# One DMA ring for the loads and the stores of an RMSNorm-SiLU kernel

## The chip, the cores and the metric

One core of a Trainium2 chip. The metric is the device time of one execution in microseconds (us). The span that a profile shows is 1.7 to 2.1 us shorter than the timed execution of the same run. All runs told here are listed as fast, but for three of the four of lockstep, which are listed as slow for their time alone: the granted clock was 1.0 in every run. Ratios are the mean time of one kernel's fast runs over that of the other kernel's fast runs of the same rounds, so they are not quite the ratios of the medians that I quote.

## The reference

```python
def reference(x, gamma, eps):                 # x: 8 x 1024 x 2048 float32, gamma: 2048
    rms = np.sqrt(np.mean(x ** 2, axis=-1, keepdims=True) + eps)
    out = gamma * x / rms
    return (out * (1 / (1 + np.exp(-out)))).astype(np.float32)
```

64 MiB come in and 64 MiB go out, and each element is touched by a handful of operations.

## The kernel before

The 8192 rows are 16 blocks of 512 rows. A block is a tile of 128 partitions with 4 rows (32 KB) each, 4 MiB in all. Six tiles rotate, so block b+6 uses the memory of block b, and its load has to wait for the store of block b.

```python
    BUFS = 6
    def load(b):
        xt = pool.tile([P, J * d], f32, name="xt")
        nc.scalar.dma_start(out=xt, in_=xb[b])          # ScalarE's queue
        blocks[b] = xt

    def squares_scalar(b, loads=()):
        ...                                              # ScalarE: Square with a row sum
                for s in loads:
                    load(s)                              # b + 3, between two squares

    def store(b):
        nc.sync.dma_start(out=ob[b], in_=blocks[b])      # SyncE's queue
    ...
        for b in range(BUFS):
            load(b)
    ...
        nc.sync.dma_start(out=grow[0:P:P // Q, :], ...)  # gamma's row
        ...                                              # TensorE spreads it, VectorE copies it to g
    ...
        for b in range(last):
            loads = [b + 3] if BUFS <= b + 3 < nblk else []
            ...                                          # squares, root, multiply, Silu, store(b)
```

ScalarE and VectorE share the squares, ScalarE takes the root and the Silu, VectorE the reciprocal and the multiplications. I call a DMA queue of one issuing engine a ring, since its transfers are served in order; load b is L(b), store b is S(b).

Of the kernel before, what the change touches and what calls it, by code (L numbers as in the profile page):

```python
# [1 line left out]

# [4 lines left out]

ACT = mybir.ActivationFunctionType
ALU = mybir.AluOpType


@with_exitstack
def kernel(
    ctx: ExitStack,
    tc: tile.TileContext,
    x: bass.AP,
    gamma: bass.AP,
    eps: bass.AP,
    out: bass.AP,
):  # L20





    nc = tc.nc
    P = nc.NUM_PARTITIONS
    f32 = mybir.dt.float32
    x2 = x.flatten_outer_dims()
    o2 = out.flatten_outer_dims()  # L30
    n, d = x2.shape
    J = 4
    BUFS = 6
    nblk = n // (P * J)
    xb = x2.rearrange("(b p j) d -> b p (j d)", p=P, j=J)
    ob = o2.rearrange("(b p j) d -> b p (j d)", p=P, j=J)

    singles = ctx.enter_context(tc.tile_pool(name="singles", bufs=1))
    pool = ctx.enter_context(tc.tile_pool(name="pool", bufs=BUFS))
    small = ctx.enter_context(tc.tile_pool(name="small", bufs=2))  # L40
    psum = ctx.enter_context(tc.tile_pool(name="psum", bufs=1, space=bass.MemoryType.PSUM))

    Q = 4
    w = d // Q
    grow = singles.tile([P, w], f32)
    g = singles.tile([P, d], f32)
    eps_t = singles.tile([P, 1], f32)
    ones = singles.tile([P, P], f32)
    junk_a = psum.tile([P, d], f32, name="junk_a")
    junk_v = psum.tile([P, d], f32, name="junk_v")  # L50
    blocks, sss, rmss, rstds = {}, {}, {}, {}

    def load(b):
        xt = pool.tile([P, J * d], f32, name="xt")
        nc.scalar.dma_start(out=xt, in_=xb[b])  # L55
        blocks[b] = xt

    def row(b, j):
        return blocks[b][:, j * d:(j + 1) * d]

    def squares_scalar(b, loads=()):


        sss[b] = small.tile([P, J], f32, name="ss")
        for j in range(share(b)):
            nc.scalar.activation(out=junk_a, in_=row(b, j), func=ACT.Square,  # L66
                                 accum_out=sss[b][:, j:j + 1])
            if j == 0:
                for s in loads:
                    load(s)  # L70

    def squares_vector(b):
        for j in range(share(b), J):
            nc.vector.tensor_tensor_reduce(  # L74
                out=junk_v, in0=row(b, j), in1=row(b, j), scale=1.0, scalar=0.0,
                op0=ALU.mult, op1=ALU.add, accum_out=sss[b][:, j:j + 1])

    def share(b):
        return 1 if 4 <= b <= 12 and b % 2 == 0 else 2

    def root(b):
        rms = small.tile([P, J], f32, name="rms")
        nc.scalar.activation(out=rms, in_=sss.pop(b), func=ACT.Sqrt, scale=1.0 / d, bias=eps_t)  # L83
        rmss[b] = rms

    def invert(b):
        rstd = small.tile([P, J], f32, name="rstd")
        nc.vector.reciprocal(out=rstd, in_=rmss.pop(b))  # L88
        rstds[b] = rstd

    def multiply(b):
        for j in range(J):
            nc.vector.scalar_tensor_tensor(out=row(b, j), in0=row(b, j), scalar=rstds[b][:, j:j + 1],  # L93
                                           in1=g, op0=ALU.mult, op1=ALU.mult)

    def silu(b):
        for h in range(0, J, 2):
            cols = slice(h * d, (h + 2) * d)
            nc.scalar.activation(out=blocks[b][:, cols], in_=blocks[b][:, cols], func=ACT.Silu)  # L99
        store(b)  # L100

    def store(b):
        nc.sync.dma_start(out=ob[b], in_=blocks[b])

    with tc.manual_schedule():

        for b in range(BUFS):
            load(b)
        nc.vector.memset(ones, 1.0)  # L109
        nc.vector.memset(eps_t, float(eps))  # L110
        nc.scalar.activation(out=junk_a[:, 0:1], in_=ones[:, 0:1], func=ACT.Square)  # L111
        nc.sync.dma_start(out=grow[0:P:P // Q, :],
                          in_=bass.AP(tensor=gamma.tensor, offset=gamma.offset, ap=[[w, Q], [1, w]]))
        for c in range(Q):
            k = c * (P // Q)
            nc.tensor.matmul(junk_v[:, c * w:(c + 1) * w], ones[k:k + 1, :], grow[k:k + 1, :],  # L116
                             start=True, stop=True)
        nc.vector.tensor_copy(out=g, in_=junk_v)  # L118



        last = nblk - 1
        SOON = 3
        squares_scalar(0)
        squares_vector(0)
        root(0)
        invert(0)
        for b in range(last):
            loads = [b + 3] if BUFS <= b + 3 < nblk else []
            if b < SOON:  # L130
                multiply(b)
                squares_scalar(b + 1, loads)
                silu(b)
                squares_vector(b + 1)
                root(b + 1)
            elif b < last - 1:
                squares_scalar(b + 1, loads)
                squares_vector(b + 1)
                root(b + 1)
                multiply(b)  # L140
                silu(b)
            else:
                multiply(b)
                squares_scalar(b + 1)
                silu(b)
                squares_vector(b + 1)
                root(b + 1)
            if b + 1 < last:
                invert(b + 1)


        for j in range(J):
            if j == J // 2:
                invert(last)
            nc.vector.tensor_mul(out=row(last, j), in0=row(last, j), in1=g)  # L155
        for j in range(J):
            nc.scalar.activation(out=row(last, j), in_=row(last, j), func=ACT.Silu,  # L157
                                 scale=rstds[last][:, j:j + 1])
        store(last)


# [1 line left out]
_INS = ['x', 'gamma', 'eps']  # L163
_OUTS = [((8, 1024, 2048), 'float32')]

_NUMBERS = {'eps': 9.999999747378752e-06}


# [26 lines left out]
```

## Time and profile before

| | before |
|---|---|
| time | 316.92 us (316.83 to 317.22); the profiled run 316.84 us |
| span in the profile | 315.1 us |
| VectorE, ScalarE busy | 75%, 68% |
| DMA engines busy, both rings | 99.0% |
| rate, over the span | 426 GB/s |

The page of the profile cuts the span into 40 slices, with a digit for the busy tenths of each engine and of the sixteen DMA engines, and the GB/s moved. The lines are in the prediction below. One more view of it matters later: the issues by kind, with the median time from issue to landing in the last column.

```profile
xt<-in_x_dram ACTq DMA_DIRECT2D x16, 4096.0 KB, 38.7
out_dram<-xt SPq DMA_DIRECT2D x16, 4096.0 KB, 29.0
```

### The profile page before, as it was taken

Reading aid. Unit: us, or ns where it says so; the run is one execution under the profiler, and the core shown is the slowest. Engines: PE = TensorE matmul, PEld = TensorE weight load, DVE = VectorE, ACT = ScalarE, POOL = GpSimd, SP = SyncE. Lnnn points to the kernel's source line nnn. Section 1 sums busy time; section 2 is a strip of 40 time slices with the busy share of each in tenths; the row PEclk is TensorE's granted clock in tenths of the full one; section 3 lists DMA queues with packets and bytes.
Section 4 is the critical chain, followed back from the end, with each engine's and each line's share of the span. In section 5 each row is a group of like instructions: output and inputs, shape, how many; then the busy total and the mean of one; then the engine's idle time right before and its main releaser. Section 6 shows DMA issues by size and latency. Waiting matters only on the chain.

```text
span 315.1 us, 436 instructions
## 1 busy us (share of the span) xinstructions
PE 2.1 (1%) x8; PEld 0.5 (0%) x8; DVE 235.3 (75%) x157; ACT 213.8 (68%) x136; POOL 0.2 (0%) x4
## 2 busy tenths in 40 slices
PE   0200000000000000000000000000000000000000
PEld 0000000000000000000000000000000000000000
DVE  0679597979995695957969489693995939999600
ACT  1349998972799258682687827877288768779910
POOL 0000000000000000000000000000000000000000
DMA  8999999999999999999999999999999999999996
GB/s 334 403 462 403 395 466 399 466 403 462 403 463 403 459 412 453 412 453 420 445 420 445 424 441 424 441 424 441 428 437 437 428 445 420 445 420 445 420 449 287
DMA packets 4618, 134.24 MB, mean 426 GB/s; under 512 B 516, under 2 KB 516, under 8 KB 520
## 3 DMA queue, kind: packets, MB, share of 16 engines
q10 hardware_dynamic: 2304, 67.11, 49.7%
q1 hardware_dynamic: 2312, 67.12, 49.3%
q14 instruction: 2, 0.02, 0.0%
HBM read 67.12 MB, written 67.11 MB: 426 GB/s over the span
## 4 chain that ended last, share of the span: by engine, by line
DMA 68%; DVE 14%; ACT 11%; issue 2%; ACTq 1%; DVEq 0%
DMA xt<-in_x_dram 68%; DVE xt L93 9%; DVE junk_v L74 5%; ACT xt L99 4%; ACT junk_a L66 3%; ACT xt L157 2%; ACT L83 1%; ACTq L190 1%; ACT L157 0%; ACT L99 0%; ACT rms L83 0%; DVE ss L74 0%; DVE rstd L88 0%; ACTq L55 0%; ACTq L83 0%
## 5 line engine op out<-in xcount | busy, mean ns | idle before, releaser
L93 DVE SCALAR_TENSOR_TENSOR xt<-xt,rstd,g 128x2048 f32<-128x2048 f32 x60 | 137.0, 2347 | 0.1
L99 ACT ACTIVATE xt<-xt 128x4096 f32<-128x4096 f32 x30 | 108.3, 3615 | 27.2 <-DVE xt L93 27.1
L74 DVE CUSTOM_DVE_ANT_0 junk_v<-xt 128x2048 f32<-128x2048 f32 x37 | 85.1, 2299 | 42.5 <-DMA xt<-in_x_dram 41.7
L66 ACT ACTIVATE junk_a<-xt 128x2048 f32<-128x2048 f32 x27 | 50.7, 1877 | 22.6 <-DMA xt<-in_x_dram 22.3
L83 ACT ACT_TABLE_LOAD x15 | 19.2, 1283 | 27.6 <-DVE ss L74 27.5
L99 ACT ACT_TABLE_LOAD x14 | 18.0, 1283 | 0.2
L118 DVE COPY g<-junk_v 128x2048 f32<-128x2048 f32 x1 | 2.3, 2292 | 9.4 <-PE junk_v L116 9.4
L88 DVE RECIPROCAL rstd<-rms 128x4 f32<-128x4 f32 x16 | 2.8, 174 | 8.3 <-ACT rms L83 8.3
L155 DVE TENSOR_TENSOR xt<-xt,g 128x2048 f32<-128x2048 f32 x4 | 8.9, 2279 | 0.0
L83 ACT ACTIVATE rms<-ss,eps_t 128x4 f32<-128x4 f32 x16 | 4.8, 297 | 5.7 <-DVE ss L74 5.5
L157 ACT ACTIVATE xt<-xt,rstd 128x2048 f32<-128x2048 f32 x4 | 7.7, 1990 | 0.0
L74 DVE DVE_READ_ACCUMULATOR2_ANT ss<- 128x1 f32 x37 | 5.2, 141 | 0.0
L66 ACT ACTIVATION_READ_ACCUMULATOR junk_a<-xt 128x1 f32 x27 | 5.0, 186 | 0.0
L111 ACT ACT_TABLE_LOAD x1 | 1.3, 1283 | 3.8 <-issue 3.8
L116 PE MATMUL junk_v<-grow,ones 1*128 1x512 f32 x8 | 2.1, 1130 | 8.2 <-DMA grow<-in_gamma_dram 8.2
L157 ACT ACT_TABLE_LOAD x1 | 1.3, 1283 | 0.0
L109 DVE MEMSET ones<- 128x128 f32 x1 | 0.2, 165 | 0.8 <-PEq L176 0.8
L116 PEld LDWEIGHTS junk_v<-grow,ones 1*128 1x128 f32 x8 | 0.5, 307 | 8.2 <-issue 8.2
L111 ACT ACTIVATE junk_a<-ones 128x1 f32<-128x1 f32 x1 | 0.2, 174 | 0.0
L176 POOL MEMSET const-bfloat16-1.0<- 128x1 bf16 x1 | 0.1, 101 | 0.0
L176 POOL MEMSET const-uint8-127<- 128x1 uint8 x1 | 0.1, 101 | 0.0
L176 POOL MEMSET const-float32-0.0<- 128x1 f32 x1 | 0.1, 98 | 0.2 <-issue 0.2
(2 smaller groups left out, 0.2 us busy)
## 6 DMA issues: line engine op xcount, KB each, us to landing
xt<-in_x_dram ACTq DMA_DIRECT2D x16, 4096.0 KB, 38.7
out_dram<-xt SPq DMA_DIRECT2D x16, 4096.0 KB, 29.0
grow<-in_gamma_dram SPq DMA_DIRECT2D x1, 8.0 KB
```

The source lines that it names most:

```text
L66: nc.scalar.activation(out=junk_a, in_=row(b, j), func=ACT.Square, accum_out=sss[b][:, j:j + 1])
L74: nc.vector.tensor_tensor_reduce(out=junk_v, in0=row(b, j), in1=row(b, j), scale=1.0, scalar=0.0, op0=ALU.mult, op1=ALU.add, accum_out=sss ...
L83: nc.scalar.activation(out=rms, in_=sss.pop(b), func=ACT.Sqrt, scale=1.0 / d, bias=eps_t)
L88: nc.vector.reciprocal(out=rstd, in_=rmss.pop(b))
L93: nc.vector.scalar_tensor_tensor(out=row(b, j), in0=row(b, j), scalar=rstds[b][:, j:j + 1], in1=g, op0=ALU.mult, op1=ALU.mult)
L99: nc.scalar.activation(out=blocks[b][:, cols], in_=blocks[b][:, cols], func=ACT.Silu)
L111: nc.scalar.activation(out=junk_a[:, 0:1], in_=ones[:, 0:1], func=ACT.Square)
L116: nc.tensor.matmul(junk_v[:, c * w:(c + 1) * w], ones[k:k + 1, :], grow[k:k + 1, :], start=True, stop=True)
L118: nc.vector.tensor_copy(out=g, in_=junk_v)
L155: nc.vector.tensor_mul(out=row(last, j), in0=row(last, j), in1=g)
L157: nc.scalar.activation(out=row(last, j), in_=row(last, j), func=ACT.Silu, scale=rstds[last][:, j:j + 1])
L190: with _tile.TileContext(nc) as tc:
```

## The change

Its intent is that ScalarE no longer issues big loads between its squares, and that loads go out as soon as their memory is free. All loads and stores go to SyncE. Behind S(b), from block 1 on, stands L(b+5), which waits for S(b-1) to land. ScalarE issues gamma's row, now straight into g without the tile grow, and nothing else.

```diff
     def load(b):
         xt = pool.tile([P, J * d], f32, name="xt")
-        nc.scalar.dma_start(out=xt, in_=xb[b])
+        nc.sync.dma_start(out=xt, in_=xb[b])
 ...
-    def squares_scalar(b, loads=()):
+    def squares_scalar(b):
 ...
-            if j == 0:
-                for s in loads:
-                    load(s)
 ...
     def store(b):
         nc.sync.dma_start(out=ob[b], in_=blocks[b])
+        if b >= 1 and b + BUFS - 1 < nblk:
+            load(b + BUFS - 1)
 ...
+        nc.scalar.dma_start(out=g[0:P:P // Q, 0:w], ...)      # gamma's row
-        nc.sync.dma_start(out=grow[0:P:P // Q, :], ...)
```

The squares, roots, multiplications and Silus keep their order.

More of the change, by code (lines that the diff above doesn't have):

```diff
@@ L44 @@
     w = d // Q
-    grow = singles.tile([P, w], f32)
     g = singles.tile([P, d], f32)
@@ L108 @@
             load(b)
+        nc.scalar.dma_start(out=g[0:P:P // Q, 0:w],
+                            in_=bass.AP(tensor=gamma.tensor, offset=gamma.offset, ap=[[w, Q], [1, w]]))
         nc.vector.memset(ones, 1.0)
@@ L111 @@
         nc.scalar.activation(out=junk_a[:, 0:1], in_=ones[:, 0:1], func=ACT.Square)
-        nc.sync.dma_start(out=grow[0:P:P // Q, :],
-                          in_=bass.AP(tensor=gamma.tensor, offset=gamma.offset, ap=[[w, Q], [1, w]]))
         for c in range(Q):
             k = c * (P // Q)
-            nc.tensor.matmul(junk_v[:, c * w:(c + 1) * w], ones[k:k + 1, :], grow[k:k + 1, :],
+            nc.tensor.matmul(junk_v[:, c * w:(c + 1) * w], ones[k:k + 1, :], g[k:k + 1, 0:w],
                              start=True, stop=True)
@@ L128 @@
         for b in range(last):
-            loads = [b + 3] if BUFS <= b + 3 < nblk else []
             if b < SOON:
                 multiply(b)
-                squares_scalar(b + 1, loads)
+                squares_scalar(b + 1)
                 silu(b)
@@ L136 @@
             elif b < last - 1:
-                squares_scalar(b + 1, loads)
+                squares_scalar(b + 1)
                 squares_vector(b + 1)
```

## The prediction

> **What bounds the kernel now.** I read the page's 40 slices first, then the queue table, then three stretches, then the waits. The first two:
>
> ```profile
> span 315.1 us, 436 instructions
> PE 2.1 (1%) x8; PEld 0.5 (0%) x8; DVE 235.3 (75%) x157; ACT 213.8 (68%) x136; POOL 0.2 (0%) x4
> ...
> DMA  8999999999999999999999999999999999999996
> GB/s 334 403 462 403 395 466 399 466 403 462 403 463 403 459 412 453 412 453 420 445 420 445 424 441 424 441 424 441 428 437 437 428 445 420 445 420 445 420 449 287
> ...
> q10 hardware_dynamic: 2304, 67.11, 49.7%
> q1 hardware_dynamic: 2312, 67.12, 49.3%
> ```
>
> The DMA row is full from the first slice to the last but one. VectorE is at 75% and ScalarE at 68%, so neither binds on average. The two queues together use 99.0% of the sixteen DMA engines' time. The saw-tooth of 403 and 466 GB/s looks like a cost of mixing reads and writes, and would be the change's prize if it were one. It isn't: the packets are of 32 KB, a slice of 7.9 us holds six or seven on each engine, and whole packets fall to one slice or the next. Longer stretches that start and end on packet bounds decide it: loads only, loads and stores mixed, stores only.
>
> ```profile
> 3.00:27.00 24.00, 2.09 (x8) 0.55 (x8) 14.44 (x10) 11.33 (x13) 0.00 (x0) 1.00 1.00 433
> 60.00:280.00 220.00, 0.00 (x0) 0.00 (x0) 176.36 (x118) 150.48 (x93) 0.00 (x0) 1.00 1.00 434
> 284.80:309.00 24.20, 0.00 (x0) 0.00 (x0) 11.63 (x9) 16.01 (x9) 0.00 (x0) 1.00 1.00 433
> ```
>
> The last two columns are DMA share and GB/s: 1.00 and 433 to 434 in all three. The rate depends neither on the direction nor on whether one queue works or two. A block is 4 MiB, 4.194 MB, and 4.194 MB / 433 GB/s = 9.68 us. The packet records of the trace say the same: consecutive completions lie 9.68 us apart in the stretches of one direction, a load and a store together take 19.36 us in between, and nearly every 32 KB packet takes 1.21 us on its engine.
>
> The waits:
>
> ```profile
> DVE junk_v L74 <- DMA xt<-in_x_dram: 41.7, 11, 5.8
> ...
> SPq L103 <- ACT xt L99: 271.4, 15, 22.2
> SPq L190 <- DMA out_dram<-xt: 12.8, 1, 12.8
> ```
>
> SyncE's queue waits 271.4 us for ScalarE's Silu. That is no loss: the stores wait, but the engines then have loads queued. VectorE waits for loads, so compute is ahead of the transfers, not behind them. The last line is the kernel's end: SyncE waits for the last store.
>
> Account of the 315.1 us: the first packet starts at 1.7 us (packet records); 32 transfers x 9.68 = 309.8; 0.7 lost on the first packets, which take 1.6 to 2.2 us in place of 1.21; 0.6 lost once, where the first store joins at about 39 us and one load packet on each engine takes 1.6 to 1.9 us; 0.7 by which the sixteen engines are staggered; about 0.4 of small change; and 1.2 from the last packet's end at 313.9 to the end of the span. Sum 315.1. The timed 316.84 is 1.7 above the profiled span.
>
> **What the Trainium skill says.** "DMA: Bandwidth & Descriptors", section "Issuing engines are not separate DMA queues": DMAs issued by ScalarE and SyncE run on the same 16 engines and interleave, and several issuers save only issue time. The trace agrees: one queue alone takes the whole 433 GB/s, and two share 434. The same page, section "Where 436 GB/s comes from", gives 435.2 GB/s as the ceiling of the fabric; the stretches lie within 0.5% of it, so no order of transfers can buy much. Its section "Queues, rings and completion order" says that an engine takes turns between queues packet by packet, and one ring in order. The trace agrees in that loads 4 and 5 took 19.4 us of engine time each beside stores and loads 1 and 2 took 9.68 alone. "HBM Reference", section "Specifications (TRN2)", gives about 425 GB/s for a core that streams alone; measured here is 2% more.
>
> **The change part by part.**
>
> *Loads move from ScalarE's queue to SyncE's.* ScalarE loses 16 issues of 0.33 to 0.55 us, about 6 us of a 68% busy engine; nothing on the path.
>
> *Packets are no longer interleaved.* The single ring holds L0 to L5, S0, S1, L6, S2, L7, S3 and so on to S10, L15, S11 to S15 (L a load, S a store). The bytes and engines stay, so 32 x 9.68 = 309.8 us stays, provided that the ring never runs dry. That is what must be worked out, since SyncE now works in order: S(b) waits for Silu of block b, and L(b+5), behind it, waits for S(b-1) to land.
>
> - Start: loads end at about 1.7 + 0.7 + 6 x 9.68 = 60.5 us. Silu 0 is done at 35.2 and Silu 1 at 49.8 in the trace, so S0 and S1 stand in the ring in time; they end at 70.2 and 79.9. L6 is issued when S0 lands, at some 72 us, 8 us before its turn. S2's Silu was done at 65.5; its turn is at 89.6.
> - Middle: L(b+5) is issued when S(b-1) lands, with L(b+4) just beginning and S(b) behind it: nearly two transfers, about 17 us, of margin. Between the landing of block b and the turn of its store lie 8 transfers, 77 us. Silu b needs block b+1 too, 19.4 us later, and about 18 us of work: about 38 us, so about 39 us of margin. The compiled order shows no further wait that could hold a SyncE issue: the other semaphores it waits for belong to transfers that ended long before.
> - End: L15 is the 27th transfer, done at 2.4 + 27 x 9.68 = 263.8 us (now about 278). From the first square on the last block to its last Silu takes 279.2 to 300.9 = 21.7 us now, so Silu 15 ends near 287; S15's turn is at 302.5. Margin 15.6 us, now about 2.3.
>
> So every margin widens or is ample, but the end is that of the ring: 2.4 + 32 x 9.68 + 0.7 = 312.9, plus up to 1 us of the small losses above, as before.
>
> *First store.* The 0.6 us loss where the first store joined a running load may go, because S0 is queued 25 us before its turn: 0 to -0.6.
>
> *Gamma's row.* ScalarE issues it in the first microsecond, as SyncE did, beside the loads on the other queue. The copy of gamma was done 0.4 us before block 0 was ready; one microsecond later would move compute by as much, and there are 25 us between Silu 0 and its store's turn. Zero.
>
> Sum: -0.3 us from the first store, my choice of half; no other term. 316.84 - 0.3 = 316.5.
>
> **Rivals.**
>
> *Each change of direction in one ring costs a bubble.* There are 21: one after L5, and two around each of L6 to L15. At the 0.6 us of the first store that makes 12.6 us, 329 us, 4% slower. For it: the trace has no ring with both directions. Against: with two queues every packet changes the direction on each engine, and those packets take 1.21 us; a boundary between two transfers of one ring costs nothing, for stores either. A bubble of 0.1 us would give about 319.
>
> *The ring runs dry*, because SyncE stands at a store while a load could go. A wait of more than 15 us beyond what I computed is needed; nothing in the trace does that. Each microsecond of dryness would be one of time. Perhaps 2%, if compute turns out slower with all loads early; it would give 320 or more.
>
> *The saw-tooth is real and unmixed traffic is faster.* The stretches of one direction ran at 433, so I see nothing to win. At the skill's 435.2 GB/s, 134.24 MB take 308.5 us, which would give about 315.5 us: the most that this could bring, still within 2%.
>
> *The start or end shrinks.* Both are latencies of the first and last transfer; the change touches neither.
>
> **Range and chances.** The lower end takes the first store's loss, part of the small losses and a little of the ceiling: 315.5. The upper takes 0.1 us for each change of direction with nothing won: 318.8. Faster by over 2% would need 310.5 us, less than the bytes need at 435.2 GB/s with start and end: 1%. Slower by over 2% needs a bubble of 0.3 us at each change of direction, or dryness: 5%.
>
> **What would show it.** In the changed profile: one queue with 134 MB and about 99% of the engines' time; 433 to 434 GB/s in stretches of several transfers; loads with a short time from issue to landing (some 20 to 30 us in place of 38.7), stores with a longer one; VectorE waiting less for loads early; SyncE's waits split between Silu and stores; the last block ready over 10 us before its store starts. I am wrong if the DMA row has slices under 9 in the middle, if packets at changes of direction take longer than 1.21 us, or if the rate exceeds 436 GB/s.

## The result, and the profile after

The changed kernel takes 320.77 us (320.15 to 321.54, 4 runs) against 316.92 us (316.83 to 317.22) of the kernel before. The ratio is 1.012, with a 95% interval of 1.0105 to 1.0135. It is slower by 3.85 us: within 2%, but outside my range of 315.5 to 318.8.

The page of the changed kernel, the lines that answer to those of before:

```profile
span 318.9 us, 447 instructions
PE 2.1 (1%) x8; PEld 0.5 (0%) x8; DVE 235.0 (74%) x157; ACT 213.4 (67%) x136; POOL 0.2 (0%) x4
...
DMA  8999999999999999999999999999999999999994
GB/s 330 423 432 452 407 456 407 382 460 407 448 419 433 437 419 440 423 436 432 427 440 423 427 423 440 448 407 448 399 440 448 411 452 415 444 427 427 456 407 185
...
q1 hardware_dynamic: 4608, 134.22, 98.4%
...
xt<-in_x_dram SPq DMA_DIRECT2D x16, 4096.0 KB, 29.9
out_dram<-xt SPq DMA_DIRECT2D x16, 4096.0 KB, 38.5
```

The DMA row is full to the end, so the ring did not run dry. Loads now land 29.9 us after their issue and stores 38.5 us, about three and four transfers of 9.68 us. In the DMA row only the last slice differs: its digit is 4 in place of 6, and 185 GB/s in place of 287.

What SyncE waits for (total us, times, longest us):

```profile
SPq L54 <- DMA out_dram<-xt: 176.4, 10, 21.8
SPq L97 <- ACT xt L93: 80.6, 6, 22.2
SPq L185 <- DMA out_dram<-xt: 26.2, 1, 26.2
```

The 271.4 us of waiting for Silu have become 80.6 for Silu and 176.4 for stores to land. The last store is issued early and the end is waited for during 26.2 us, where it was 12.8. So the schedule does what it was meant to do, and the end is later all the same.

Stretches tell where. First the kernel before (the last two columns are DMA share and GB/s):

```profile
60.00:230.00 170.00, 0.00 (x0) 0.00 (x0) 135.10 (x93) 113.02 (x71) 0.00 (x0) 1.00 1.01 435
230.00:280.00 50.00, 0.00 (x0) 0.00 (x0) 41.26 (x26) 37.46 (x23) 0.00 (x0) 1.00 1.00 430
...
311.00:313.00 2.00, 0.00 (x0) 0.00 (x0) 0.00 (x0) 0.00 (x0) 0.00 (x0) 1.00 0.72 311
313.00:315.00 2.00, 0.00 (x0) 0.00 (x0) 0.00 (x0) 0.00 (x0) 0.00 (x0) 1.00 0.00 0
```

The same view of the changed kernel:

```profile
60.00:230.00 170.00, 0.00 (x0) 0.00 (x0) 142.49 (x97) 120.82 (x74) 0.00 (x0) 1.00 1.00 428
230.00:280.00 50.00, 0.00 (x0) 0.00 (x0) 43.25 (x27) 39.06 (x25) 0.00 (x0) 1.00 1.01 436
284.80:309.00 24.20, 0.00 (x0) 0.00 (x0) 2.14 (x1) 6.55 (x4) 0.00 (x0) 1.00 1.00 433
...
313.00:315.00 2.00, 0.00 (x0) 0.00 (x0) 0.00 (x0) 0.00 (x0) 0.00 (x0) 1.00 0.42 180
315.00:317.00 2.00, 0.00 (x0) 0.00 (x0) 0.00 (x0) 0.00 (x0) 0.00 (x0) 1.00 0.15 66
```

Two things are to be seen. Between 60 and 230 us the rate is 428 and not 435 GB/s, at a DMA share of 1.00: an engine whose packet takes longer counts as busy, so the loss is in the GB/s column and not in the busy share. The ends of a stretch cut through packets, which moves such a figure by some GB/s, as the 430 and 436 of the 50 us after it show; from 60 to 280 us the rate is 430 in the change and 434 before. And in the last microseconds the share falls to 0.42 and then 0.15 of sixteen engines: a few engines still work when the others are done.

The records of the trace below these views confirm it. Each transfer runs on all sixteen engines, and each engine signals its own completion. The records name no engine; one is followed by the packet that starts where another ended. This is how far the last completion of a transfer lies behind the first one, worked out from those signals:

```
us between the first and the last of 16 completions
          L5    L6    L7    L8    L9    L10   L11   L12   L13   L14   L15   S15
before   0.41  0.66  1.10  1.08  1.06  1.07  1.04  1.01  1.00  0.99  0.99  0.97
changed  0.52  0.88  1.33  1.92  2.38  3.05  3.33  3.45  4.31  4.28  4.27  4.29
```

The first completion of the last store comes at 313.79 us in place of 313.29, 0.5 us later. The last one lies 4.29 us behind it in place of 0.97, 3.3 us more. Together these are the 3.8 us of the span. Nine of the sixteen engines lie within 0.45 us of the first, and six are 1.5 to 4.3 us behind.

The packet records say at which packets an engine falls behind. At 58 to 60 us, where the ring turns from L5 to S0, the last load packets take up to 2.1 us in place of 1.21 on every engine; a typical engine loses 0.95 us there and 0.2 us at the next turn, against 0.6 us where the first store joined in the kernel before. This is the 0.5 us. After that nearly all packets of over 1.3 us are the last load packet of an engine ahead of a store: at 89 to 90, 109, 129, 148, 168, 188, 207 and 226 us, on some engines and not on others, with 1.3 to 2.1 us. At the last two turns, at 246 and 266 us, there is one such packet each, and the table shows no more growth. Where the ring turns from a store to a load, or two transfers of one direction follow each other, such packets are rare: two, at 98.6 and 121.6 us.

The first of these two most likely has another cause. It starts where a packet of 8 KB ended with which the program fetches instructions (98.3 us, queue q14). The kernel before has two of them, at 94.0 and 108.8 us, and the packets behind them take 1.33 and 1.57 us; the steps to 0.66 and 1.10 us in the table come right after them. They are not the cause of the loss: copy_one_ring, below, has none after its start and its engines drift 4.70 us apart.

### The profile page after: what moved, and what is told of

The parts are those of the page before. It is cut to its first block, busy times and chain, and to the rows that moved or that the text cites. A ratio compares the mean times of both kernels' runs of the same rounds, so it can differ in the third digit from the quotient of the medians.

```text
span 318.9 us, 447 instructions
## 1 busy us (share of the span) xinstructions
PE 2.1 (1%) x8; PEld 0.5 (0%) x8; DVE 235.0 (74%) x157; ACT 213.4 (67%) x136; POOL 0.2 (0%) x4
## 4 chain that ended last, share of the span: by engine, by line
DMA 53%; DVE 22%; ACT 11%; issue 4%; ACTq 1%; SPq 0%
DMA out_dram<-xt 37%; DMA xt<-in_x_dram 16%; DVE xt L87 13%; DVE junk_v L68 9%; ACT xt L93 4%; ACT junk_a L63 3%; ACT xt L152 2%; ACT L77 2%; ACTq L185 1%; ACT L152 0%; ACT L93 0%; ACT rms L77 0%; SPq L54 0%; DVE ss L68 0%; DVE rstd L82 0%
## 5 line engine op out<-in xcount | busy, mean ns | idle before, releaser
L68 DVE CUSTOM_DVE_ANT_0 junk_v<-xt 128x2048 f32<-128x2048 f32 x37 | 85.0, 2297 | 33.2 <-DMA xt<-in_x_dram 32.4
L63 ACT ACTIVATE junk_a<-xt 128x2048 f32<-128x2048 f32 x27 | 50.6, 1876 | 22.1 <-DMA xt<-in_x_dram 21.7
L112 PE MATMUL junk_v<-g,ones 1*128 1x512 f32 x8 | 2.1, 1132 | 8.3 <-DMA g<-in_gamma_dram 8.3
## 6 DMA issues: line engine op xcount, KB each, us to landing
xt<-in_x_dram SPq DMA_DIRECT2D x16, 4096.0 KB, 29.9
out_dram<-xt SPq DMA_DIRECT2D x16, 4096.0 KB, 38.5
```

The source lines that it names most:

```text
L63: nc.scalar.activation(out=junk_a, in_=row(b, j), func=ACT.Square, accum_out=sss[b][:, j:j + 1])
L68: nc.vector.tensor_tensor_reduce(out=junk_v, in0=row(b, j), in1=row(b, j), scale=1.0, scalar=0.0, op0=ALU.mult, op1=ALU.add, accum_out=sss ...
L112: nc.tensor.matmul(junk_v[:, c * w:(c + 1) * w], ones[k:k + 1, :], g[k:k + 1, 0:w], start=True, stop=True)
```

## The experiments

**Theory A**: a turn from loads to stores inside one ring makes some engines fall behind, 3.85 us / 11 turns = 0.35 us a turn in what sets the end. **Rival B**: it is the moment at which the loads go out, whatever ring they stand in. **Rival C**: any boundary between two transfers of a ring costs. All kernels of a call share their runs of the kernel before, which took 316.89 to 316.95 us.

### Two rings again, nothing else undone (two_rings)

```diff
     def store(b):
-        nc.sync.dma_start(out=ob[b], in_=blocks[b])
+        nc.scalar.dma_start(out=ob[b], in_=blocks[b])
         if b >= 1 and b + BUFS - 1 < nblk:
             load(b + BUFS - 1)
```

> The changed kernel with one edit: ScalarE issues the stores, SyncE the loads, so that loads and stores stand in two rings again while each load still waits for the same store as in the change. Theory A (each change from loads to stores inside one ring costs some engines time; 3.85 us over 11 such changes is 0.35 us each): the loss is gone, 316.5 to 317.2 us, and the sixteen completions of the last store lie about 1 us apart as in the kernel before (4.3 us in the change). Theory B (the order and the moment of the loads cost the time, whatever ring they stand in): it stays at 320 to 321.5 us.

317.45 us (317.33 to 317.69), ratio 1.0015 (1.0000 to 1.0030). Its stretches:

```profile
60.00:230.00 170.00, 0.00 (x0) 0.00 (x0) 134.75 (x93) 113.11 (x71) 0.00 (x0) 1.00 1.01 434
313.00:315.00 2.00, 0.00 (x0) 0.00 (x0) 0.00 (x0) 0.00 (x0) 0.00 (x0) 1.00 0.00 0
```

The rate is back at 434, nothing is left after 313 us, and the completions of the last store lie 0.96 us apart. 3.3 of the 3.85 us are gone. B falls. The remaining 0.5 us, a little more than A allowed, is at the edge of the interval; the profiled span is only 0.1 us longer than before (315.2 against 315.1), so most of it lies outside the span. Its cause stays open.

### Fewer turns: pairs

```diff
         nc.sync.dma_start(out=ob[b], in_=blocks[b])
-        if b >= 1 and b + BUFS - 1 < nblk:
-            load(b + BUFS - 1)
+        if b % 2 == 1:
+            for s in (b + BUFS - 1, b + BUFS):
+                if s < nblk:
+                    load(s)
```

> One ring, but two stores and then two loads in turn (S2 S3 L8 L9 S4 S5 L10 L11 ...), so 6 changes from load to store in place of 11. Theory A: 316.9 + 6 x 0.35 = about 319.0 us (318.3 to 319.7). Theory B (moment of the loads): 320.5 us or more, as every second load is issued later than in the change.

319.24 us (318.80 to 319.35), ratio 1.0068 (1.0053 to 1.0083), with completions of the last store 3.04 us apart. It is A's number.

### More turns: halves that take turns, and halves that don't

From S0 and L6 on every transfer is cut in two by columns. In halves_mixed the order is

```diff
-        nc.sync.dma_start(out=ob[b], in_=blocks[b])
-        if b >= 1 and b + BUFS - 1 < nblk:
-            load(b + BUFS - 1)
+        store_half(b, 0)
+        if more: load_half(s, 0)        # s = b + BUFS - 1
+        store_half(b, 1)
+        if more: load_half(s, 1)
```

and in halves_apart both halves of the store come first.

> One ring; from load 6 and store 0 on each transfer is cut in two of 2 MiB (16 KB runs) and halves of a store and of a load take turns: 21 changes from load to store in place of 11, the same bytes. Theory A: 316.9 + 21 x 0.35 = about 324 us (322.5 to 326), clearly over halves_apart. Theory B: like halves_apart.

> The control of halves_mixed: the same halves, but both of a store and then both of a load, so 11 changes from load to store as in the change. Theory A: about 320.8 us plus what 16 KB runs cost (0 to 2 us). Rival C (every boundary between two transfers of a ring costs, with or without a change of direction): this one is slower than the change by as much as halves_mixed is.

halves_mixed took 321.22 us (321.14 to 321.35), ratio 1.0134 (1.0117 to 1.0151); halves_apart 321.78 us (320.78 to 322.29), ratio 1.0147 (1.0127 to 1.0167). The control came as expected, but 21 turns cost no more than 11. A's fixed price for each turn falls here. In halves_mixed the completions drift apart up to about 3.56 us at some 160 us and stay there for the rest, over more than ten further turns; in halves_apart they reach 4.47 us. C falls as well: halves_apart has twice the boundaries of the change and is only 1.0 us slower, and of that 0.7 us is in the engines that don't fall behind (first completion of the last store at 314.49 us in place of 313.79), which looks like the price of 16 KB packets.

### Stores in both rings, and two rings that turn together

In odd_stores ScalarE issues the stores of even blocks; in stores_pool GpSimd issues all stores; in lockstep every transfer is two halves by partitions, one from each of SyncE and GpSimd.

```diff
# odd_stores
-        nc.sync.dma_start(out=ob[b], in_=blocks[b])
+        (nc.sync if b % 2 else nc.scalar).dma_start(out=ob[b], in_=blocks[b])
# stores_pool
+        nc.gpsimd.dma_start(out=ob[b], in_=blocks[b])
# lockstep, the loads likewise
+        nc.sync.dma_start(out=ob[b][:P // 2, :], in_=blocks[b][:P // 2, :])
+        nc.gpsimd.dma_start(out=ob[b][P // 2:, :], in_=blocks[b][P // 2:, :])
```

> The changed kernel, but ScalarE issues the stores of even blocks: SyncE's ring holds all loads and the odd stores (6 changes from load to store, as in pairs), ScalarE's ring the even stores, so that for most of the time an engine serves two rings and reads and writes are mixed over the sixteen engines. Theory A1 (a change inside a ring costs, whatever else goes on): about 319 us, like pairs. A2 (what costs is that all engines turn from loading to storing at about the same time) and A3 (a change inside a ring costs only where no other ring has work): 316.5 to 317.7 us, and the completions of the last store within about 1 us.

> Control for lockstep: the change with all stores issued by GpSimd, loads by SyncE. As two_rings, 317.0 to 318.5 us, unless GpSimd as issuer costs by itself; by how much it is over two_rings (317.45) is then to be taken off lockstep.

> Every transfer of the change in two halves by partitions (0-63 and 64-127, still 32 KB runs), SyncE issuing the one and GpSimd the other in the same order: two rings that both turn from loads to stores at the same time, 11 changes each. A1 and A2: about 320 to 321.5 us, with the completions of the last store 3 us or more apart. A3: about 317 to 318 us. GpSimd's own cost as an issuer is in the control stores_pool.

odd_stores took 321.77 us (320.92 to 323.12), ratio 1.0153 (1.0120 to 1.0187), more than each of the three had said. A2 and A3, which left no room for a loss, fall as they stood: a second ring that often has stores to serve does not hide it. A1 has the right sign and too small a number. The trace shows packets of 1.4 to 2.2 us where the first even store joins an engine that had only loads, at 37 to 39 us, as in the kernel before, and more such packets later; the completions of the last store lie 4.73 us apart. My reading after the fact is that a store which joins such an engine from the other ring counts as a turn too, and here that happens again and again, as the ring of even stores runs empty in between. That was not tried by itself.

stores_pool took 317.59 us (317.49 to 317.64), ratio 1.0020 (1.0005 to 1.0035): like two_rings. It does not matter here whether ScalarE or GpSimd issues the stores, only that it is another engine than that of the loads.

lockstep took 443.15 us in its one fast run (up to 469.83 in the three slow ones) and failed as an experiment. The page of the fast run:

```profile
GB/s 191 220 211 235 196 232 196 232 199 229 253 381 307 297 422 294 389 309 366 336 336 383 285 425 261 422 306 407 330 395 339 389 342 342 392 333 354 345 267 27
```

Already in the first quarter, with loads alone, it moves about half of 433 GB/s, and its 32 KB packets take 2.4 us in the median in place of 1.21. The halves are slow before any turn, so the question of two rings turning together stays open. The Trainium skill advises against such a split: "DMA: Bandwidth & Descriptors", section "Rules for kernel authors", says of two transfers to disjoint partition halves that they serialize, and to use one transfer of 128 partitions. The 191 to 235 GB/s of the loads here fit that advice.

### The transfers alone

All compute is taken out, which makes the result wrong on purpose; each store waits only for its load. None, three, five or eleven turns are then easy to arrange.

```diff
# copy_one_ring: order and ring of the change
-        squares_scalar(0)
-        ...
-        store(last)
+        for b in range(nblk):
+            store(b)
# copy_two_rings: as copy_one_ring, and
+        nc.scalar.dma_start(out=ob[b], in_=blocks[b])
# copy_threes (G = 3) and copy_sixes (G = 6): one ring, G stores, then G loads
+        if b % G == G - 1:
+            for s in range(b + 1 - G + BUFS, b + 1 + BUFS):
+                if s < nblk:
+                    load(s)
```

> Wrong result on purpose: the change without its compute (no squares, root, multiply, Silu), the same loads and stores in the same ring and order, each store waiting only for its load. If the loss is a matter of the transfers alone: 320 to 321.5 us, completions of the last store 3 to 5 us apart. If compute's traffic in SBUF makes it (rival): 316.5 to 317.5 us and about 1 us apart.

> Wrong result on purpose: transfers alone as in copy_one_ring (321.12 us), but ScalarE issues the stores, so loads and stores stand in two rings that are both filled nearly all the time. If the loss belongs to turning one ring from loads to stores: 316.3 to 317.5 us, completions of the last store about 1 us apart. If transfers without compute are slower for a reason of their own: as copy_one_ring.

> Wrong result on purpose: transfers alone, one ring, three stores and three loads in turn: 5 changes from loads to stores in place of 11. If each change costs about as much, (321.12 - 316.9) / 11 = 0.38 us: 316.9 + 5 x 0.38 = 318.8 us (318.0 to 319.5). If the first change or two make the whole loss: 320 to 321 us.

> Wrong result on purpose: as copy_threes with groups of six, so 3 changes from loads to stores: 316.9 + 3 x 0.38 = 318.0 us (317.3 to 318.6) if each change costs about as much; 320 to 321 us if one ring costs by itself or the first change makes it all.

| transfers alone | turns in a ring | us | ratio (interval) | completions of S15 apart, us |
|---|---|---|---|---|
| copy_two_rings | none | 316.89 (316.26 to 317.22) | 0.9994 (0.9976 to 1.0011) | 1.05 |
| copy_sixes | 3 | 316.91 (316.79 to 317.33) | 0.9999 (0.9984 to 1.0014) | 0.73 |
| copy_threes | 5 | 319.08 (317.09 to 319.46) | 1.0052 (1.0019 to 1.0086) | 2.86 |
| copy_one_ring | 11 | 321.12 (320.67 to 321.33) | 1.0130 (1.0115 to 1.0145) | 4.70 |

The stretches of copy_one_ring:

```profile
60.00:230.00 170.00, 0.00 (x0) 0.00 (x0) 0.00 (x0) 0.00 (x0) 0.00 (x0) 1.00 1.00 429
313.00:315.00 2.00, 0.00 (x0) 0.00 (x0) 0.00 (x0) 0.00 (x0) 0.00 (x0) 1.00 0.31 131
315.00:317.00 2.00, 0.00 (x0) 0.00 (x0) 0.00 (x0) 0.00 (x0) 0.00 (x0) 1.00 0.19 82
```

and of copy_two_rings:

```profile
60.00:230.00 170.00, 0.00 (x0) 0.00 (x0) 0.00 (x0) 0.00 (x0) 0.00 (x0) 1.00 1.01 435
313.00:315.00 2.00, 0.00 (x0) 0.00 (x0) 0.00 (x0) 0.00 (x0) 0.00 (x0) 1.00 0.00 0
```

With VectorE and ScalarE idle the rate again falls from 435 to 429 GB/s and again a few engines are late at the end. So compute has no part in the loss; one ring by itself costs nothing either, as copy_sixes shows; from 3 to 5 to 11 turns the loss grows. Three turns cost less than in proportion: copy_sixes missed my 318.0 us. Two limits: the loss does not come in every run, as one of the four runs of copy_threes took 317.09 us and the others 319.05 to 319.46. And fewer turns mean longer groups of loads and stores here; no run parts the two, and halves_mixed shows that the number of turns alone does not decide.

### Gamma's part (gamma_alone)

```diff
# the kernel before, with
-        nc.sync.dma_start(out=grow[0:P:P // Q, :], ...)
+        nc.scalar.dma_start(out=grow[0:P:P // Q, :], ...)
```

> The kernel before with one part of the change: ScalarE issues gamma's row, behind its six loads, not SyncE. The row lands some microseconds later, or a whole load queue later if it stands behind the loads in their ring: then g is ready only after about 60 us and the start of compute is put off by about 47 us; the stores then start late, and the end may move by some microseconds. If the row goes past the loads: 316.9 us. This order of issue isn't that of the change (there the loads are in the other ring), so it tells why the change could not have kept the loads on ScalarE with gamma behind them, rather than a cost of the change.

355.93 us (355.71 to 356.04), ratio 1.1229: 39 us more, and not the "some microseconds" that I had expected. The first of these two lines is TensorE's wait for gamma's row, the second the DMA row of the page:

```profile
PE junk_v L116 <- DMA grow<-in_gamma_dram: 61.7, 1, 61.7
...
DMA  8999998002855899999999999999999999999997
```

The 8 KB row stood behind six loads in one ring, compute began a load queue later, and with all six tiles full the DMA engines had nothing to do for two slices. In the change the row is in the other ring than the loads, as it was before: TensorE waits 8.3 us there and 8.2 us in the kernel before. So this part of the change costs nothing, but only because the loads moved away from ScalarE at the same time.

### Why just a few engines: a stagger made on purpose

Three more runs went to one question: does an engine fall behind at a turn because it is already behind? A small first load gives four engines a packet more.

```diff
+        nc.sync.dma_start(out=blocks[1][0:4, :], in_=xb[1][0:4])    # 4 partitions x 32 KB
         ...                                                          # then L0, L1 and so on
```

> Wrong result on purpose: copy_sixes, but a first small load of 4 partitions x 32 KB gives four of the sixteen engines one packet of 1.21 us more, so that they trail the other twelve by that from the start; 3 turns from loads to stores. If trailing engines lose more at each turn: clearly more than 316.9 + 1.2 = 318.1 us, 318.8 to 320.5, with four completions of the last store 2.5 us or more behind. If the place of an engine doesn't matter: 317.8 to 318.4 us, and the four 1.2 to 1.8 us behind.

> The change with the same small first load: four engines trail by 1.2 us, 11 turns. If trailing engines lose more: these four and at most one or two others fall behind in the first turns, the other twelve stay within about 0.7 us of each other (in the change, five to seven engines lie 0.9 to 4.3 us behind), and the time is 320.5 to 322.5 us. If the place doesn't matter: stragglers among the twelve as in the change, and 321.5 to 322.5 us.

> Control: two_rings (317.45 us) with the same small first load. No turns in a ring: 318.2 to 319.0 us, the four engines 1.2 to 2 us behind from the first load to the last store, without growth.

copy_sixes_stagger took 320.74 us (320.57 to 321.25), after_stagger 323.95 us (323.23 to 324.50), two_rings_stagger 321.13 us (321.12 to 321.34). All three lie above their ranges. The first is above the range of "trailing engines lose more", and without the control I would have taken it for a proof. The control shows that the small load alone costs 321.13 - 317.45 = 3.7 us: the first packets of all engines take 3.1 to 4.1 us beside it, where they took 1.6 to 2.2. Against that, 320.74 - 316.91 = 3.8 and 323.95 - 320.77 = 3.2 us leave nothing for a dearer turn, if the small load costs as much in one ring as in the control's two. In copy_sixes_stagger the four engines go from 1.1 to 1.5 us behind in the first load to 1.8 to 1.9 in the last store. In after_stagger the four last completions go from 1.3 to 1.7 us to 3.9 to 4.7 us behind, and three of the other twelve also fall 0.9 to 2.0 us behind. So the time does not bear the theory out, and the places do so at most in part. Why some engines pay at a turn and others not stays open, and so does why the drift stops growing in halves_mixed (3.56 us) and in the change (4.3 us) while the ring goes on turning.

No kernel tried is faster than the kernel before by more than its runs scatter.

## Why the prediction was wrong, point by point

- **What bounds the kernel.** Right. The transfers set the end in the kernel before and in the change: with the compute removed the times differ by under 0.6 us (321.12 against 320.77 in one ring, 316.89 against 317.45 in two).
- **The ring does not run dry.** Right, with its numbers: loads land 29.9 us after issue (I had said 20 to 30), VectorE's wait for loads falls from 41.7 to 32.4 us, and the last Silu ends at 291.3 us with its store's turn some 13 us later (I had said 15.6). L15 landed only at 269.7 us, where I had 263.8, since its last engine was behind. The small error in my sum, 263.8 + 21.7 being 285.5 and not "near 287", does not matter here.
- **Gamma and the start.** Right: 8.3 us of waiting against 8.2.
- **"Packets are no longer interleaved ... 32 x 9.68 = 309.8 us stays".** This is the step that failed. It holds for ten of the engines, not for the slowest: with 11 turns the last store's last completion lies 4.3 us behind its first, and the kernel ends with its slowest engine. I worked with one rate for sixteen engines and so had no term for engines that drift apart; the account of the kernel before had it as "0.7 by which the sixteen engines are staggered", taken over into the sum for the change as if it were fixed. There the term measured 4.3 us. The sign of being wrong that I had named came with it: packets at the turns took 1.3 to 2.1 us in place of 1.21.
- **The first store's loss, "0 to -0.6".** Wrong in sign. The turn from L5 to S0 costs a typical engine 0.95 us, where the first store cost 0.6 us before.
- **The rival "each change of direction in one ring costs a bubble".** This is what happened, and I gave slower by over 2% only 5% and put its small version, 0.1 us a turn, at the edge of my range. What I held against it, that packets of two rings alternate without cost, is true (copy_two_rings, 316.89 us) but is not about one ring. I had seen the one case of loads followed by a first store, 0.6 us on every engine, and should have trusted it as evidence. The size is 3.85 / 11 = 0.35 us a turn in the change, but not a price by the piece: 3 turns cost 0.0, 5 turns 2.2, 6 turns 2.3, 11 turns 3.9 to 4.2 us, and 21 turns of half the length 4.3 us, with 16 KB packets included. The first turn is in all of these counts, though the kernel before pays 0.6 us for its first store too. And only the 11 changes from loads to stores showed long packets, not the 10 back that the rival's 21 included.

## What to carry to other kernels

When a kernel is bound by its transfers, keep the loads in one ring and the stores in another, or let one ring turn seldom: a ring that turns from loads to stores eleven times cost 1.2% here, one that turns three times cost nothing, and two rings that are both filled ran at the full rate. Compare completions engine by engine, since a DMA share of 1.00 can hide packets that take longer, and the slowest of sixteen engines sets the end. And put a small transfer that everything waits for in the ring that is not full of large ones.

## What the Trainium skill lacked or had wrong

- "DMA: Bandwidth & Descriptors", section "Rules for kernel authors", says that spreading DMAs over several issuers doesn't help the bandwidth. For loads and stores that take turns this was wrong here: the same transfers took 321.12 us in one ring that turns eleven times and 316.89 us in two rings, without any compute. With three turns one ring was as fast as two (316.91 us).
- No page speaks of a ring that turns from loads to stores: packets of 1.3 to 2.1 us in place of 1.21 at the turns, and engines up to 4.3 us apart at the end.
- No page says that a small load to 4 partitions at the head of a ring slows the first packets of all sixteen engines: they took 3.1 to 4.1 us beside it in place of 1.6 to 2.2, and the kernel took 3.7 us longer.
